# First feature tiles of a hybrid pooling and state-space block: conditioning product shared with TensorE, low parts of weights on VectorE, copies on ScalarE, written order of VectorE

## The chip, the cores and the metric

The kernel runs on one core of one Trainium2 chip. The metric is the device time of one execution in microseconds (us), the lower the better. A profile shows the span from the first to the last instruction of one execution.

## The reference, cut to what matters

The block is a decoder layer with adaptive normalization. What the change touches is the first projection and the modulation ahead of it; all is float32, with 1024 tokens and a width of 1024.

```python
c_act = silu(c)
mod = einsum('bd,de->be', c_act, w_ada) + b_ada          # 1024 -> 6 x 1024
shift_m, scale_m, gate_m, shift_f, scale_f, gate_f = split(mod, 6)
u = rms_norm(h, g_mix) * (1.0 + scale_m) + shift_m
proj = einsum('bsd,de->bse', u, w_in)                    # pooling, z, xBC, dt
...                                                       # pooling and SSD mixers, w_out
u = rms_norm(h, g_mlp) * (1.0 + scale_f) + shift_f
h = h + gate_f * (square(relu(u @ w_up)) @ w_down)
```

## The kernel before, in words

**High and low parts.** A float32 product is made of three products in a shorter format. Each operand is split into a high part (a cast) and a low part (the operand less the high part). `mm3` (L244) multiplies high by high, high by low and low by high into one bank of PSUM. The high part of a weight tile is cast by ScalarE in `unit` (L194). Its low part is a subtraction (L195), on GpSimd when `ring["pool_lo"]` is set and on VectorE otherwise.

**The stage.** The change concerns the loop over eight blocks of 128 input channels, called chunks 0 to 7 here. In chunk k, six output tiles of 128 features (B, C and four x tiles) take the first 512 tokens: 6 x 3 = 18 matmuls of 128x512 into six banks that stay open through all chunks. Chunk k needs the modulated input `u` of block k as high and low part, and the weight tile k (128x768) as high and low part. Two buffers each hold raw weight tiles, their high parts and their low parts, so the parts of tile k+2 overwrite those of tile k.

**The conditioning product.** `u` needs the shift and the scale of block k, which are 256 columns of `w_ada`. `ada_load` brings a tile of 1024x256 (1 MB) into one of three buffers, as eight slices of 128 rows. `ada_reduce` on VectorE multiplies slice j by its column of silu(c) and adds, into two accumulators (L264 for the first two slices, L266 for the other six). `ada_dve` adds the two accumulators (L358), and `ada_pe` sums over partitions on TensorE with a column of ones (L364). `ada_cols` makes shift and scale from that on VectorE (L368, L369). Then `ada_u` calls `split_u`: the high part on ScalarE (L252), the same value in float32 on VectorE (L256), and the low part on VectorE (L257).

**The order.** A planner puts each engine's instructions in order by its own costs. Under `pinned` the named engines keep the order in which the program is written. `AP[k]` says before which of the six tiles of chunk k the conditioning of block k+1 is put, and `CUTS[k]` says how many slices of block k+2 are reduced ahead of it. `stage_x` transposes the block of x for k+2 on TensorE and copies it out on ScalarE; `SX0` and `SX` give its place. After the matmuls of chunk k the next weight tile, k+2, is requested. In chunk 5 the first two of the units that follow (z and dt columns, 512 wide) are requested too, then rows 4 to 7 of x. `XS` says in which chunk those rows are normalized: rows 4 and 5 are scaled on GpSimd (L501), 6 on VectorE, 7 on ScalarE. After the stage come the z and dt products, the convolutions and the other halves of the tiles.

Of the kernel before, what the change touches and what calls it, by code (L numbers as in the profile page):

```python
# [9 lines left out]
F32 = mybir.dt.float32  # L10
F32R = mybir.dt.float32r
BF16 = mybir.dt.bfloat16
AF = mybir.ActivationFunctionType
# [4 lines left out]
P = 128  # L18
S = 1024
D = 1024  # L20
# [15 lines left out]
EPS = 1e-5  # L36
UM = 544
WARM = 7
CUTS = (0, 4, 4, 4, 4, 4, 4, 4)
UACT = ()  # L40
AP = (5, 2, 2, 2, 2, 2, 2)
UH = ((), (0,), (1, 2), (3, 4), (5, 6, 7))
XK = 5
NPF = 2
XS = {5: (4,), 6: (5, 6), 7: (7,)}
WARM2 = 2
XWB = 1
Z0 = 240
# [3 lines left out]
FIN2 = 8.0  # L52
N20 = 10.0
SX0 = 1
SX = 1
PK = 2
N21 = 15.6
G21 = 1.6
# [11 lines left out]
def tile_hybrid_block(  # L70
# [133 lines left out]
    def prefetch(n):  # L204
        while specs and len(ready) < n:
            kn, ncol, parts, gate = specs.popleft()
            ready.append(unit(kn, ncol, parts, gate() if gate is not None else None))
# [65 lines left out]
    def feat_specs(off):  # L273
        for i in range(2):
            specs.append((4, P, [(0, P, win_r[:, 4 * i:4 * i + 4, off:off + P])], None))
# [39 lines left out]
    def utmp():  # L315
        return stp.tile([P, HW], F32, name="utmp", tag="utmp", bufs=2)
# [23 lines left out]

    def ada_load(k):
        t = stp.tile([P, KD, 256], F32, name="adaw", tag="adaw", bufs=3)
        n = 4 if k == 0 else 1
        w = KD // n
        for j in range(n):
            ks = slice(j * w, (j + 1) * w)
            for f in range(2):
                sp.dma_start(out=t[:, ks, f * P:(f + 1) * P], in_=wada_r[:, ks, f * D + k * P:f * D + (k + 1) * P])
        ada_w[k] = t

    ada_a = {}

    def ada_dve(k, ks=range(KD)):
        if ks.start == 0:
            ada_a[k] = [stp.tile([P, 256], F32, name="adaa", tag="adaa", bufs=4) for _ in range(2)]
        ada_reduce(ada_w[k], ada_a[k], 256, ks)
        if ks.stop == KD:
            dve.tensor_tensor(out=ada_a[k][0], in0=ada_a[k][0], in1=ada_a[k][1], op=ALU.add)  # L358

    def ada_pe(k):  # L360
        ps = bank()
        pa, pb = ps[:, 0:1], ps[:, 1:2]
        for f, p_ in enumerate((pa, pb)):
            pe.matmul(p_, lhsT=ada_a[k][0][:, f * P:(f + 1) * P], rhs=ones[:, 0:1], start=True, stop=True)  # L364
        ada_cols(k, pa, pb)

    def ada_cols(k, pa, pb):
# [3 lines left out]
                                 in1=pc[:, C_GMIX + k:C_GMIX + k + 1], op0=ALU.add, op1=ALU.mult)  # L371

    def ada_u(k):
        uT[k][0] = split_u(stage.pop(k), sc_m[:, k:k + 1], sh_m[:, k:k + 1], utmp(), k in UACT)

    stage = {}

# [8 lines left out]
    with pinned((act, dve, pool, pe)):  # L386
# [45 lines left out]
        row_scale(3, False, slice(0, HW))  # L432
        row_scale(3, True, slice(HW, D))
        dve_f0(range(2, KD))
        dve.tensor_tensor(out=acc[0], in0=acc[0], in1=acc[1], op=ALU.add)
        for i in range(3):
            pe_f1(range(2 * i, 2 * i + 2))
            busy(2)
        stage_x(0)
        pe_f1(range(6, KD))  # L440
        pe.matmul(pa, lhsT=acc[0], rhs=ones[:, 0:1], start=True, stop=True)
        ada_cols(0, pa, pb)
        ada_u(0)
        pool.tensor_tensor(out=lo0, in0=raw0, in1=hi0.bitcast(F32), op=ALU.subtract)
        stage_x(1)
        busy(WARM2)
        kw.append([(hi0, lo0)])
# [7 lines left out]
        pool.dma_start(out=nea, in_=a_log.broadcast_to([P, HEADS]))  # L455
        pool.dma_start(out=dsk, in_=d_skip.broadcast_to([P, HEADS]))

    ring["pool_lo"] = True
    kw.append(get(1, 0))
    accs = [bank() for _ in range(6)]  # L460
    for k in range(KD):
        if k + 2 < KD:
            ada_load(k + 2)
        if k == 0:
            ada_dve(1)
        whi, wlo = kw[k][0]
        u = uT[k][0]
        for f in range(6):
            if f == (SX0 if k < 2 else SX) and k + 2 < KD:
                stage_x(k + 2)  # L470
            if k + 1 < KD and f == AP[k]:
                cut = CUTS[k]
                with pinned((dve,)):
                    if cut and k + 2 < KD:
                        ada_dve(k + 2, range(cut))
                    ada_pe(k + 1)
                    ada_u(k + 1)
                    if k + 2 < KD:
                        ada_dve(k + 2, range(cut, KD))
            fs = slice(f * P, (f + 1) * P)  # L480
            mm3(accs[f], whi[:, fs], wlo[:, fs], (u[:, 0, :], u[:, 1, :]), k == 0, k == KD - 1)
        if k == PK:
            params()
        if k + 2 < KD:
            kw.append(get(1, 0))
        if k == 5:
            ring["now"] = (unitm, unitm, UM, 4, 6)
            ring["pool_lo"] = False
            for i in range(4):
                specs.append((2, 256, [  # L490
                    (0, Z0, win_r[:, 2 * i:2 * i + 2, OFF_Z:OFF_Z + Z0]),
                    (Z0, 256, win_r[:, 2 * i:2 * i + 2, OFF_DT:OFF_DT + HEADS])], None))
            feat_specs(G1[0][0])
        if k == XK:
            prefetch(NPF)
            for t in range(4, 8):
                sp.dma_start(out=tok[:, t, :], in_=x_r[:, t, :])
        for t in XS.get(k, ()):
            row_rs(t, pool)
            if t < 6:  # L500
                pool.tensor_tensor(out=tok[:, t, :], in0=tok[:, t, :], in1=rst[:, t:t + 1].broadcast_to([P, D]),  # L501
                                   op=ALU.mult)
            else:
                row_scale(t, t == 7)
    prefetch(6)
    ring["pool_lo"] = True
    st.close()
# [1019 lines left out]
```

## Time and profile before

| | before |
|---|---|
| median of 3 runs | 1175.19 us (1174.83 to 1176.52) |
| profiled execution | 1176.13 us, span 1174.4 us |
| TensorE busy | 1138.9 us, 97% of the span |
| VectorE busy | 837.2 us, 71% |
| ScalarE busy | 558.5 us, 48% |
| GpSimd busy | 191.5 us, 16% |
| mean granted TensorE clock | 0.991 |

The profiled execution is 1.73 us longer than its span and 0.94 us above the median. A busy share over the whole span is a mean over stages. The stage of the change lies between 16.7 and 77 us, where TensorE was busy for 48.97 of 60.3 us at a mean granted clock of 0.89.

### The profile page before, as it was taken

How to read it: one execution, taken by the hardware profiler on the slowest of the kernel's cores; microseconds unless marked ns; L12 is line 12 of the kernel's file. 1: busy time of each engine (PE TensorE's matmuls, PEld its weight loads, DVE VectorE, ACT ScalarE, POOL GpSimd, SP SyncE). 2: the span in 40 equal slices, each digit the busy share in tenths (PEclk: the TensorE clock that was granted, in tenths of full speed). 3: DMA queues.
4: the chain of work that ended last, by engine and by line, in shares of the span. 5: the costliest groups of instructions: out<-in, count | busy, mean ns of one | idle time of the engine just before them, and what ended most of it. 6: DMA issues, size and time to landing. Idle time of an engine off the chain costs nothing.

```text
span 1174.4 us, 15348 instructions
## 1 busy us (share of the span) xinstructions
PE 1138.9 (97%) x5569; PEld 946.2 (81%) x5569; DVE 837.2 (71%) x1232; ACT 558.5 (48%) x977; POOL 191.5 (16%) x214
## 2 busy tenths in 40 slices
PE   6889999999999999999999999999999999999997
PEld 5678787777799988887778888888888888888886
DVE  6968879967978746664887766666566844586985
ACT  4266566544433633544764444444444444335363
POOL 4233446524500011122000000000100000000030
PEclk9989999999999999999999999999999999999999
DMA  9831342233357645853146343442399934775732
GB/s 288 234 112 37 81 137 91 73 94 103 109 186 220 201 155 172 277 170 135 37 182 237 118 189 128 168 152 108 122 388 362 338 108 151 242 250 198 268 126 90
DMA packets 124876, 200.73 MB, mean 171 GB/s; under 512 B 8416, under 2 KB 67584, under 8 KB 122752
## 3 DMA queue, kind: packets, MB, share of 16 engines
q1 hardware_dynamic: 123440, 196.24, 50.0%
q0 software_dynamic: 1120, 3.21, 0.8%
q8 instruction: 43, 0.70, 0.2%
q10 hardware_dynamic: 240, 0.30, 0.1%
q14 instruction: 33, 0.27, 0.1%
HBM read 159.81 MB, written 39.91 MB: 170 GB/s over the span
## 4 chain that ended last, share of the span: by engine, by line
PE 86%; DVE 7%; DMA 2%; ACT 2%; issue 1%; SPq 1%; POOL 1%; POOLq 0%; ACTq 0%; DVEq 0%
PE bank L244 78%; DVE cv L542 3%; PE bank L720 2%; PE bank L138 1%; PE bank L724 1%; PE bank L717 1%; DMA raw<-in_w_in_dram 1%; DMA adaw<-in_w_ada_dram 1%; DVE adaa L266 1%; PE bank L796 1%; PE bank L1003 1%; DMA tok<-in_x_dram 1%; DVE cv L553 1%; DVE lo L195 0%; POOL tok L953 0%
## 5 line engine op out<-in xcount | busy, mean ns | idle before, releaser
L244 PE MATMUL bank<-u,hi 128*128 128x512 f32 x560 | 186.2, 414 | 2.1 <-ACT u L252 2.0
L244 PE MATMUL bank<-dhi 128*128 128x512 f32 (+1 forms) x452 | 175.1, 387 | 1.1 <-DVE tmp L1423 1.1
L244 PE MATMUL bank<-dlo,dhi 128*128 128x512 f32 (+1 forms) x452 | 175.0, 387 | 0.0
L244 PE MATMUL bank<-dhi,dlo 128*128 128x512 f32 (+1 forms) x452 | 175.0, 387 | 0.0
L244 PEld LDWEIGHTS bank<-u,hi 128*128 128x128 f32 x560 | 105.3, 192 | 30.1 <-issue 5.0
L1358 DVE TENSOR_TENSOR dlo<-fr,dhi 128x1024 fp32r<-128x1024 f32 x56 | 68.4, 1222 | 82.4 <-ACT dhi L1357 82.3
L244 PE MATMUL bank<-hi,ym 128*128 128x512 f32 x384 | 125.4, 400 | 0.0
L1357 ACT CAST dhi<-fr 128x1024 fp32r<-128x1024 f32 x56 | 58.9, 1052 | 139.2 <-PE bank L244 103.9
L244 PE MATMUL bank<-u,lo 128*128 128x512 f32 x280 | 111.3, 397 | 0.0
L194 ACT CAST hi<-raw 128x512 fp32r<-128x512 f32 (+2 forms) x109 | 67.8, 630 | 91.4 <-PE bank L244 70.2
L195 DVE TENSOR_TENSOR lo<-raw,hi 128x512 fp32r<-128x512 f32 (+1 forms) x87 | 65.1, 759 | 49.7 <-ACT hi L194 49.0
L244 PEld LDWEIGHTS bank<-dhi 128*128 128x128 f32 x452 | 84.8, 188 | 18.8 <-DVE tmp L1423 1.3
L244 PEld LDWEIGHTS bank<-dhi,dlo 128*128 128x128 f32 x452 | 84.9, 188 | 17.3
L244 PEld LDWEIGHTS bank<-dlo,dhi 128*128 128x128 f32 x452 | 84.9, 188 | 17.2
L244 PE MATMUL bank<-hi,u 128*128 128x256 f32 (+1 forms) x512 | 98.2, 289 | 0.1
L179 POOL TENSOR_TENSOR rst<-ssq,mhalf 128x1 f32<-128x1 f32 (+2 forms) x27 | 27.4, 1015 | 399.5 <-DVE ssq L178 374.3
L244 PE MATMUL bank<-E,whl 128*128 128x512 f32 x384 | 91.6, 389 | 0.0
L244 PEld LDWEIGHTS bank<-hi,ym 128*128 128x128 f32 x384 | 72.1, 188 | 16.4 <-issue 0.7
L244 PEld LDWEIGHTS bank<-E,whl 128*128 128x128 f32 x384 | 72.1, 188 | 15.0
L244 PEld LDWEIGHTS bank<-hi,u 128*128 128x128 f32 x512 | 81.0, 191 | 1.3 <-issue 0.7
L244 PE MATMUL bank<-u,whl 128*128 128x512 f32 x312 | 75.2, 389 | 0.9 <-ACT whl L1137 0.9
L244 PE MATMUL bank<-lo,ym 128*128 128x512 f32 x192 | 75.3, 392 | 0.0
(254 smaller groups left out, 2159.7 us busy)
## 6 DMA issues: line engine op xcount, KB each, us to landing
f_d<-tok SPq DMA_DIRECT2D x16, 1792.0 KB, 7.2
wr<-in_w_down_dram SPq DMA_DIRECT2D x56, 512.0 KB, 5.3
fr<-f_d SPq DMA_DIRECT2D x53, 512.0 KB, 4.2
raw<-in_w_ada_dram SPq DMA_DIRECT2D x64, 256.0 KB, 3.1
wraw<-in_w_up_dram SPq DMA_DIRECT2D x16, 1024.0 KB, 5.4
raw<-in_w_in_dram SPq DMA_DIRECT2D x48, 256.0 KB, 3.0
raw<-in_w_out_dram SPq DMA_DIRECT2D x48, 256.0 KB, 3.1
tok<-in_x_dram SPq DMA_DIRECT2D x16, 512.0 KB, 6.0
```

What stands on the lines that cost most here:

```text
L138: return pe.transpose(dst, src, ident)
L179: pool.tensor_tensor(out=rst[:, a:b], in0=m, in1=mhalf[:, :b - a], op=ALU.pow)
L194: act.copy(hi[:, :n], raw[:, :n])
L195: (pool if ring.get("pool_lo") else dve).tensor_tensor(out=lo[:, :n], in0=raw[:, :n], in1=hi[:, :n].bitcast(F32), op=ALU.subtract)
L244: pe.matmul(ps, lhsT=st_, rhs=mv, start=first and i == 0, stop=last and i == 2, skip_group_check=more)
L266: dve.scalar_tensor_tensor(out=a, in0=view[:, k, :n], scalar=cact[:, k:k + 1], in1=a, op0=ALU.mult, op1=ALU.add)
L542: dve.scalar_tensor_tensor(out=v, in0=cr[:, k:k + HW], scalar=pw[:, 12 * k + ct:12 * k + ct + 1], in1=v, op0=ALU.mult, op1=ALU.add)
L553: dve.scalar_tensor_tensor(out=v, in0=th, scalar=1.0, in1=v, op0=ALU.add, op1=ALU.mult)
L717: pe.matmul(po, lhsT=C[:, cs], rhs=states[g], start=True, stop=True)
L720: pe.matmul(py[:, hh * HD:(hh + 1) * HD], lhsT=Ms[hh // 4][:, (hh % 4) * P:(hh % 4 + 1) * P], rhs=xdt[:, hh * HD:(hh + 1) * HD], start=Tru ...
L1357: act.copy(hi, src)
L1358: dve.tensor_tensor(out=lo, in0=src, in1=hi.bitcast(F32), op=ALU.subtract)
```

## The change

- `ADA_PE` takes slices of the conditioning product from VectorE to TensorE: slices 4 to 7 for blocks 1 and 2, slices 6 and 7 for block 3. TensorE multiplies each slice by a column of silu(c) into the same PSUM column.
- The sum of the two accumulators (L358, and L435 for block 0) is gone. TensorE multiplies both accumulators by ones into the same column.
- Low parts of the weight tiles 0 to 7 are made on VectorE, not on GpSimd.
- `ada_hi` and `ada_lo` take the place of `ada_u` for blocks 1 to 7. The float32 copy of `u` is on VectorE for blocks 1 to 3 (`TDVE`) and on ScalarE for blocks 4 to 7.
- The written order of VectorE now covers the whole of chunks 0 to 5, low parts of weights included, with other values of `CUTS` and `AP`. In chunks 3 to 5 the rest of the reduction stands between `ada_hi` and `ada_lo`.
- The transposes of x for blocks 4 to 7 come one tile later (`SX` 2). The load of block 1 is issued in four pieces, not in two. Rows 4 and 5 are scaled on VectorE, one chunk later for row 4, and rows 4 to 7 are divided between chunks 6 and 7.

```diff
-CUTS = (0, 4, 4, 4, 4, 4, 4, 4)
-UACT = ()
-AP = (5, 2, 2, 2, 2, 2, 2)
+CUTS = (0, 0, 0, 2, 4, 4, 0)
+TDVE = (1, 2, 3)
+AP = (4, 1, 1, 1, 1, 1, 1)
+ADA_PE = {1: (4, 5, 6, 7), 2: (4, 5, 6, 7), 3: (6, 7)}
-XS = {5: (4,), 6: (5, 6), 7: (7,)}
+XS = {6: (4, 5), 7: (6, 7)}
-SX = 1
+SX = 2
-        n = 4 if k == 0 else 1
+        n = (4, 2)[k] if k < 2 else 1
-    def ada_dve(k, ks=range(KD)):
-        if ks.start == 0:
+    def ada_dve(k, ks):
+        ks = [j for j in ks if j not in ADA_PE.get(k, ())]
+        if not ks:
+            return
+        if ks[0] == 0:
             ada_a[k] = [stp.tile([P, 256], F32, name="adaa", tag="adaa", bufs=4) for _ in range(2)]
         ada_reduce(ada_w[k], ada_a[k], 256, ks)
-        if ks.stop == KD:
-            dve.tensor_tensor(out=ada_a[k][0], in0=ada_a[k][0], in1=ada_a[k][1], op=ALU.add)
         for f, p_ in enumerate((pa, pb)):
-            pe.matmul(p_, lhsT=ada_a[k][0][:, f * P:(f + 1) * P], rhs=ones[:, 0:1], start=True, stop=True)
+            fs = slice(f * P, (f + 1) * P)
+            for j in ADA_PE.get(k, ()):
+                pe.matmul(p_, lhsT=ada_w[k][:, j, fs], rhs=cact[:, j:j + 1], start=j == ADA_PE[k][0], stop=False)
+            for i in range(2):
+                pe.matmul(p_, lhsT=ada_a[k][i][:, fs], rhs=ones[:, 0:1], start=k not in ADA_PE and i == 0,
+                          stop=i == 1)
+    def ada_hi(k):
+        u = uT[k][0] = actp.tile([P, 2, HW], F32R, name="u", tag="a")
+        tmp, src = utmp(), stage.pop(k)
+        act.activation(out=u[:, 0, :], in_=src, func=AF.Identity, scale=sc_m[:, k:k + 1], bias=sh_m[:, k:k + 1])
+        if k in TDVE:
+            dve.tensor_scalar(out=tmp, in0=src, scalar1=sc_m[:, k:k + 1], scalar2=sh_m[:, k:k + 1],
+                              op0=ALU.mult, op1=ALU.add)
+        else:
+            act.activation(out=tmp, in_=src, func=AF.Identity, scale=sc_m[:, k:k + 1], bias=sh_m[:, k:k + 1])
+        return tmp
+    def ada_lo(k, tmp):
+        u = uT[k][0]
+        dve.tensor_tensor(out=u[:, 1, :], in0=tmp, in1=u[:, 0, :].bitcast(F32), op=ALU.subtract)
-        dve.tensor_tensor(out=acc[0], in0=acc[0], in1=acc[1], op=ALU.add)
+        dve.tensor_tensor(out=lo0, in0=raw0, in1=hi0.bitcast(F32), op=ALU.subtract)
-        pe.matmul(pa, lhsT=acc[0], rhs=ones[:, 0:1], start=True, stop=True)
+        for i in range(2):
+            pe.matmul(pa, lhsT=acc[i], rhs=ones[:, 0:1], start=i == 0, stop=i == 1)
-        pool.tensor_tensor(out=lo0, in0=raw0, in1=hi0.bitcast(F32), op=ALU.subtract)
-    ring["pool_lo"] = True
-                with pinned((dve,)):
-                    if cut and k + 2 < KD:
-                        ada_dve(k + 2, range(cut))
-                    ada_pe(k + 1)
-                    ada_u(k + 1)
-                    if k + 2 < KD:
-                        ada_dve(k + 2, range(cut, KD))
+                ada_dve(k + 2, range(cut))
+                ada_pe(k + 1)
+                tmp = ada_hi(k + 1)
+                if cut:
+                    ada_dve(k + 2, range(cut, KD))
+                ada_lo(k + 1, tmp)
+                if not cut and k + 2 < KD:
+                    ada_dve(k + 2, range(KD))
-            if t < 6:
-                pool.tensor_tensor(out=tok[:, t, :], in0=tok[:, t, :], in1=rst[:, t:t + 1].broadcast_to([P, D]),
-                                   op=ALU.mult)
-            else:
-                row_scale(t, t == 7)
+            row_scale(t, t == 7)
+    with pinned((dve,)):
+        ada_dve(1, range(KD))
+        for k in range(6):
+            chunk(k)
+    chunk(6)
+    chunk(7)
```

## Rows read from the trace of the kernel before

**Rows 1.** Windows: length, busy of PE PEld DVE ACT POOL, clock, DMA, GB/s.

```profile
16.70:77.00 60.30, 48.97 (x208) 38.55 (x209) 49.50 (x96) 21.00 (x35) 23.00 (x21) 0.89 0.75 211
...
25.60:33.85 8.25, 6.85 (x26) 5.39 (x26) 7.67 (x18) 2.67 (x5) 1.88 (x1) 0.79 1.07 292
...
47.41:54.19 6.78, 5.48 (x29) 4.17 (x27) 6.35 (x14) 2.02 (x4) 2.03 (x1) 1.00 0.93 258
```

**Rows 2.** Waits between 16.7 and 77 us: total, times, longest.

```profile
PE bank L364 <- DVE adaa L358: 9.6, 5, 2.9
```

**Rows 3.** Timeline of chunk 5, VectorE: start, duration, instruction.

```profile
47.38 0.69 DVE L257 TENSOR_TENSOR u<-utmp,u 128x512 fp32r<-128x512 f32 x1 [0.36 <-ACT u L252]
47.99 3.26 DVE L266 SCALAR_TENSOR_TENSOR adaa<-adaw,cact,adaa 128x256 f32<-128x256 f32 x4
51.29 0.42 DVE L358 TENSOR_TENSOR adaa<-adaa 128x256 f32<-128x256 f32 x1
51.63 0.61 DVE L264 TENSOR_SCALAR adaa<-adaw,cact 128x256 f32<-128x256 f32 x2
52.16 0.87 DVE L266 SCALAR_TENSOR_TENSOR adaa<-adaw,cact,adaa 128x256 f32<-128x256 f32 x2
52.95 0.15 DVE L368 TENSOR_TENSOR sh_m<-bank,pc 128x1 f32<-128x1 f32 x1
...
53.26 0.55 DVE L256 TENSOR_SCALAR utmp<-stage,sc_m,sh_m 128x512 f32<-128x512 f32 x1
```

**Rows 4.** Line L266, all of the stage: duration in ns, min/median/max.

```profile
L266 DVE SCALAR_TENSOR_TENSOR adaa<-adaw,cact,adaa x42: 470/479/2075, 19.2 to 64.3; 128x256 f32<-128x256 f32 x42
```

**Rows 5.** Timeline of TensorE in chunk 5, and GpSimd beside it.

```profile
48.15 2.03 POOL L195 TENSOR_TENSOR lo<-raw,hi 128x768 fp32r<-128x768 f32 x1 [3.96 <-ACT hi L194]
...
49.14 0.40 PE L244 MATMUL bank<-u,lo 128*128 128x512 f32 x1
...
50.07 0.40 PE L244 MATMUL bank<-u,lo 128*128 128x512 f32 x1
...
53.71 0.60 PE L138 MATMUL bank<-ident,tok 128*128 128x128 f32 x4
54.19 0.50 PE L244 MATMUL bank<-u,hi 128*128 128x512 f32 x1
```

**Rows 6.** Timeline of TensorE, chunks 0 and 1, and the end of the stage.

```profile
23.76 0.58 PE L364 MATMUL bank<-ones,adaa 128*128 128x1 f32 x4 [2.75 <-DVE adaa L358]
...
28.07 0.63 PE L244 MATMUL bank<-u,hi 128*128 128x512 f32 x1
28.49 0.63 PE L244 MATMUL bank<-u,lo 128*128 128x512 f32 x1
...
69.87 0.41 PE L244 MATMUL bank<-hi,u 128*128 128x256 f32 x1
...
72.22 1.80 PE L244 MATMUL bank<-u,hi 128*128 128x512 f32 x4
```

**Rows 7.** Timeline of weight loads, block 0: products with a slice of w_ada.

```profile
13.19 0.53 PEld L428 LDWEIGHTS bank<-cact,adaw 128*128 128x128 f32 x4
13.64 0.53 PEld L333 LDWEIGHTS bank<-ones,ident 128*128 128x128 f32 x4
```

**Rows 8.** Low parts on VectorE elsewhere: duration in ns, min/median/max.

```profile
L195 DVE TENSOR_TENSOR lo<-raw,hi x6: 676/682/693, 64.7 to 81.0; 128x512 fp32r<-128x512 f32 x6
...
L1358 DVE TENSOR_TENSOR dlo<-fr,dhi x56: 1214/1224/1227, 855.5 to 1150.6; 128x1024 fp32r<-128x1024 f32 x56
```

**Rows 9.** Timeline of ScalarE in chunk 5.

```profile
53.32 0.81 ACT L252 ACTIVATE u<-stage,sh_m,sc_m 128x512 fp32r<-128x512 f32 x1 [4.76 <-DVE sc_m L369]
54.04 0.82 ACT L194 CAST hi<-raw 128x768 fp32r<-128x768 f32 x1
```

**Rows 10.** Chain of waits near the end of the stage: start, duration, piece.

```profile
56.40 7.92 DMA raw<-in_w_in_dram
```

**Rows 11.** Windows behind the stage, columns as in Rows 1.

```profile
92.00:135.00 43.00, 42.92 (x248) 37.30 (x247) 37.65 (x63) 25.80 (x48) 17.81 (x22) 1.00 0.21 56
```

More of the change, by code (lines that the diff above doesn't have):

```diff
@@ L373, in ada_u @@
     def ada_u(k):
-        uT[k][0] = split_u(stage.pop(k), sc_m[:, k:k + 1], sh_m[:, k:k + 1], utmp(), k in UACT)
+        uT[k][0] = split_u(stage.pop(k), sc_m[:, k:k + 1], sh_m[:, k:k + 1], utmp(), False)
+    def ada_hi(k):
[11 more added lines that the diff above has]
+        dve.tensor_tensor(out=u[:, 1, :], in0=tmp, in1=u[:, 0, :].bitcast(F32), op=ALU.subtract)
     stage = {}
@@ L456, in tile_hybrid_block, with chunk @@
         pool.dma_start(out=dsk, in_=d_skip.broadcast_to([P, HEADS]))
-    ring["pool_lo"] = True
     kw.append(get(1, 0))
     accs = [bank() for _ in range(6)]
-    for k in range(KD):
+    def chunk(k):
         if k + 2 < KD:
             ada_load(k + 2)
-        if k == 0:
-            ada_dve(1)
         whi, wlo = kw[k][0]
@@ L493, in tile_hybrid_block @@
             feat_specs(G1[0][0])
+            prefetch(NPF)
         if k == XK:
-            prefetch(NPF)
             for t in range(4, 8):
```

## The prediction, made before the changed kernel was run

> **What bounds the kernel now.** I first read the windows over the stage [rows 1]. The first feature tiles run from 16.7 to 77 us. In these 60.3 us TensorE is busy for 48.97 and VectorE for 49.50, and the granted clock is 0.89 on average. One chunk of the middle shows which of the two sets the pace: in 6.78 us TensorE has 5.48 us of work at clock 1.00, while VectorE's 6.35 us of merged busy time leave only the gap in which it waits for ScalarE's high part. The list of waits then names the place [rows 2]: five times, 9.6 us in all, TensorE stands at the conditioning sum (L364) until VectorE has added its two accumulators (L358).
>
> The timeline of that chunk shows VectorE's round, 47.38 to 54.16 [rows 3]. Its largest piece is four reductions that take 3.26 us, while two of them take 0.79 us (52.16 to 52.95) further on. The extreme duration of the same line is 2075 ns against a median of 479 [rows 4], and it falls beside GpSimd's low part of the weights, 2.03 us long [rows 5]. So GpSimd's work, meant to relieve VectorE, holds it up for about 1.6 us a chunk. The DMA queues come last in the reading: they were full, at 292 GB/s, for part of the stage [rows 1], but the list names no DMA among TensorE's waits.
>
> **How much there is to get.** At full clock a 128x512 matmul follows the one before it after (50.07 - 49.14) / 4 = 0.233 us, and four transposes take 54.19 - 53.71 = 0.48 us [rows 5]. Two conditioning products, four weight loads, take 13.64 - 13.19 = 0.45 us [rows 7]. The stage needs 8 x 18 x 0.233 = 33.6 us of matmuls, 6 x 0.48 = 2.9 of transposes, and 7 x 0.45 = 3.2 for 14 conditioning products. The eleven 128x256 matmuls of the next stage that the planner put inside took 72.22 - 69.87 = 2.35 us [rows 6] at the slow clock, so half of that, 1.2, at the fast one. That is 40.9 us out of 60.3. The other 19.4 are idle time and matmuls at the lower level, 1.2 GHz, where the spacing is 28.49 - 28.07 = 0.42 us [rows 6].
>
> **What the change adds on TensorE.** Blocks 1 to 7 take 12, 12, 8 and four times 4 conditioning products, 48 in place of 14. The 34 more cost 34 x 0.225 = 7.65 us, nothing hides them, and TensorE is to be the pace setter. Taken from the busy time of the same row (0.53 us for two) [rows 7] they would cost 9.0. Block 0's second product, one more in the start-up, is dropped as small. 19.4 - 7.65 = 11.75 us remain if TensorE then never waits.
>
> **VectorE's new round.** For blocks 4 to 7 it holds eight reductions, 52.16 - 51.63 = 0.53 for the first two and 6 x 0.40 for the rest, 2.9 us in all. The shift and scale take 53.26 - 52.95 = 0.31 us and the low part of `u` 47.99 - 47.38 = 0.61 [rows 3]. New is the low part of a 128x768 weight tile. The trace has it at 128x512 for 0.68 us and at 128x1024 for 1.22 [rows 8]; I take the middle, 0.95. The sum is 4.8 us, where before it was 6.78: gone are the addition (51.63 - 51.29 = 0.34), the float32 copy and the 1.6 us of blocking. Blocks 1 to 3 keep the copy, 0.55 us [rows 3], but give two or four reductions of 0.40 to TensorE, so they lie at 4.6 or below. TensorE's own round in chunks 3 to 5 is 4.19 + 0.48 + 0.90 = 5.57 us. VectorE fits under it with 0.8 us to spare; that spare time covers the low part's price, and at 1.22 it still would.
>
> **ScalarE** gets the float32 copy for blocks 4 to 7, like L252 at 0.81 us [rows 9]. It has 2.0 us of work in 6.78 [rows 1], so I cost the four copies at nothing as load. They lengthen one chain: low part of `u` later by 0.81. VectorE spends that time in the second half of the reduction (1.6 us), which covers it.
>
> **The new wait.** VectorE now makes the low part of weight tile k+2 itself. That must wait until TensorE is through with chunk k, which frees the buffer, and until ScalarE has cast the high part (0.82 us) [rows 9]. Queued behind it on VectorE are the shift and scale of block k+2 and all reductions, and TensorE waits for both. The circle in chunks 4 to 6 is: chunk 5.57, cast 0.82, low part 0.95, first half of the reduction 1.3, shift and scale 0.31, second half 1.6, low part of `u` 0.61. That is 11.2 us for two chunks, 5.6 a chunk, just above 5.57. So it nearly closes without loss, but every late step shows.
>
> **Stalls that stay.** Into chunk 1: 0.31 + 0.81 + 0.61 = 1.73 us of chain behind the sum, with six matmuls (1.4 us) to cover it, 0.35 lost. In chunk 3, TensorE comes to the sum of block 4 while its eight reductions, which start only after the low part of block 3, are running: 0.4. The circle, three chunks with 0.2 each for gaps between instructions: 0.6. Eight changes of chunk at 0.1: 0.8, an estimate by the gaps between dependent instructions in VectorE's round. Together 2.15 us. Both ends: 0.5 if the planner fills them with later matmuls, as it did before, and 5 if each of the seven rounds is late by 0.7.
>
> **Parts at nothing.** In the start-up VectorE takes the low part of weight tile 0 and loses the addition and a GpSimd neighbour: between a loss of 0.95 and a gain of about as much, taken as zero. Scaling rows 4 and 5 on VectorE costs two instructions, where GpSimd's blocked an addition for about as long; it lies beside the last chunks. Load pieces: the second half of a 1 MB load costs SP two more issues, covered by queues already full at that point. Moving the transposes one tile later costs nothing while four stage buffers are ahead. A chunk's loads are 1.05 + 0.39 MB, 4.9 us at 292 GB/s [rows 1]: under 5.57, so the DMA doesn't set the pace, but it is next in line.
>
> **Sum.** 11.75 - 2.15 = 9.6 us. From the profiled execution's 1176.13 that makes 1166.5. It lies 0.94 above the median of 1175.19, so against the median the forecast is 1165.6 us. Behind the stage, between 92 and 135 us, TensorE is busy for 42.92 of 43.0 us [rows 11], so what is gained ahead of it should arrive at the end. The forecast's own range, by 9.0 for the products and 0.5 to 5 us of stalls, is 1164 to 1170.
>
> **Rivals.**
>
> Clock falls behind the thin products (chance 0.17). Before, TensorE idled for 2.75 us and then ran four instructions of one column [rows 6]. The next window had a granted clock of 0.79 [rows 1], and about ten matmuls at 0.42. The change puts 12 products in a row, 2.7 us with almost no columns, into chunks 0 and 1, and 1.8 us into chunk 2. Against it: they do keep the engine issuing. Two to three falls of ten to twelve matmuls at 0.19 us more make 4 to 6 us: 1170.5. The Trainium skill ("TensorE: Matmul & The Clock Gate", "What's actually happening") says that the fast clock has to be earned by recent TensorE activity and the slow one is the default. By that rule I would expect these falls if thin products don't count as activity; the idle stretch above agrees with it, and no row shows what products alone do.
>
> Late raw tiles at the end (0.15). VectorE's written order ends chunk 5 with the low parts of two z units. Their raw tiles needed 7.92 us to land before [rows 10]. If they land 3 us after VectorE arrives and block 7's shift stands behind them, chunk 7 waits 3 us, and matmuls at the low clock behind it cost 2 more: 1170.6. My walk through the rounds puts VectorE there about 2 us after they land.
>
> The clock stays low through chunks 0 to 3 (0.06): the other side. All 72 matmuls there at 0.42 cost 72 x 0.19 = 13.7 us, 4.1 more than the gain: 1179.3. It decides from 9.6 / 0.19 = 50 matmuls. Against it: the clock came back behind the 2.75 us gap, and the window of chunk 5 has it at 1.00 [rows 1], with a gap in each chunk.
>
> The gain is given back behind the stage (0.07): VectorE is busy for 37.65 of 43 us there [rows 11], and its convolutions could set the time however early the tiles come: 1175, or a little over with the planner's other order.
>
> **Chances and range.** The forecast has 0.55. Faster than the median by over 0.2%, which is about what a measurement of this kernel can tell from no change: 0.55 + 0.17 + 0.15 = 0.87. Within it: 0.05, most of the last rival. Slower: 0.06 + 0.02 = 0.08. The range reaches from 1161.5, where the planner fills every gap and the start-up gains too, to 1172.5, which takes in the two rivals at 1170.5 and leaves out the last two.
>
> **What would show it.** Right: the stage's tiles end near 67 us; TensorE's waits at L364's successor sum to under 2.5 us; reductions stay near 479 ns, none near 2 us; a round lasts 5.6 us; the clock is 1.00 in chunks 3 to 7. Wrong: matmuls spaced by 0.42 in chunks 1 and 2; VectorE waiting for the cast (L194) by more than 0.8 us a chunk; products at more than 0.27 us; or the stage early and the convolutions no earlier.

## The result, and the profile after

| | before | after |
|---|---|---|
| median of 16 runs each (lowest, highest), us | 1176.37 (1174.13, 1177.45) | 1169.26 (1165.20, 1175.31) |
| profiled execution, us | 1176.13 | 1170.18 |
| span, us | 1174.4 | 1168.3 |
| VectorE busy, us | 837.2 | 823.9 |
| GpSimd busy, us | 191.5 | 169.7 |

The ratio is 0.9942 [0.9929, 0.9956]: faster by 0.6%, 7.1 us between the medians where 9.6 were forecast. The executions of the changed kernel scatter far more than those of the one before. Seven lie between 1165.2 and 1166.2, six between 1168.8 and 1171.3, three between 1173.3 and 1175.3. The profiled one is of the middle group.

The lines of the changed kernel are one higher, and further on by more: `mm3` is L245, the low part of a weight tile L196, the reductions L265 and L267, the slice products L368, the sum over the accumulators L370, shift and scale L375 and L376, the high part of `u` L386, its low part L396. First the windows (columns as in [rows 1]): the stage, two rounds of VectorE in its second half, and the stretch behind it.

```profile
16.70:77.00 60.30, 59.71 (x348) 52.02 (x347) 40.47 (x97) 31.78 (x52) 5.29 (x12) 1.00 0.81 223
...
47.30:52.65 5.35, 4.99 (x28) 3.98 (x27) 5.35 (x16) 2.84 (x4) 0.00 (x0) 1.00 0.84 219
52.65:57.50 4.85, 4.85 (x29) 4.14 (x28) 4.75 (x14) 2.83 (x4) 0.00 (x0) 1.00 1.03 261
92.00:135.00 43.00, 42.92 (x236) 36.94 (x236) 39.50 (x63) 24.98 (x48) 20.09 (x24) 1.00 0.26 68
```

In the 60.3 us of [rows 1] TensorE is now busy for 59.71 and VectorE for 40.47, where both had about 49. The list of waits over the stage says the same: the wait of [rows 2], 9.6 us, is gone, TensorE has 0.6 us of waits left up to 75 us, and VectorE is now the one that waits (total, times, longest).

```profile
DVE sh_m L375 <- PE bank L370: 11.5, 4, 5.7
...
PE bank L245 <- ACT u L386: 0.4, 1, 0.4
PE bank L245 <- DVE lo L196: 0.2, 1, 0.2
```

The reductions have lost the long one of [rows 4] (ns, min/median/max), and the low part of a weight tile at 128x768 is now on VectorE:

```profile
L267 DVE SCALAR_TENSOR_TENSOR adaa<-adaw,cact,adaa x32: 476/481/483, 20.6 to 58.9; 128x256 f32<-128x256 f32 x32
...
L196 DVE TENSOR_TENSOR lo<-raw,hi x9: 686/954/959, 28.0 to 63.2; 128x768 fp32r<-128x768 f32 x7, 128x512 fp32r<-128x512 f32 x2
```

One round of VectorE, to be held against [rows 3] (start, duration, instruction):

```profile
47.29 0.16 DVE L375 TENSOR_TENSOR sh_m<-bank,pc 128x1 f32<-128x1 f32 x1
...
47.48 2.46 DVE L267 SCALAR_TENSOR_TENSOR adaa<-adaw,cact,adaa 128x256 f32<-128x256 f32 x6
49.85 0.69 DVE L396 TENSOR_TENSOR u<-utmp,u 128x512 fp32r<-128x512 f32 x1
50.46 0.95 DVE L196 TENSOR_TENSOR lo<-raw,hi 128x768 fp32r<-128x768 f32 x1
51.33 0.61 DVE L265 TENSOR_SCALAR adaa<-adaw,cact 128x256 f32<-128x256 f32 x2
51.85 0.88 DVE L267 SCALAR_TENSOR_TENSOR adaa<-adaw,cact,adaa 128x256 f32<-128x256 f32 x2
52.65 0.15 DVE L375 TENSOR_TENSOR sh_m<-bank,pc 128x1 f32<-128x1 f32 x1
```

Six reductions take 49.85 - 47.48 = 2.37 us, 0.40 each, where four took 3.26. The round is 52.65 - 47.29 = 5.36 us and holds ten multiplications of slices (L265 and L267 together); the next, with eight, is 57.49 - 52.65 = 4.84.

**Where the time went.** For the bookkeeping I cut each profiled execution at two marks: the first 128x512 feature matmul, and the end of the last one of the stage. The time from the start of the span to the first mark is the start-up, between them lies the stage, and the rest is what lies behind.

| profiled execution | start-up | stage | TensorE waits in it | behind | time |
|---|---|---|---|---|---|
| before | 16.74 | 60.55 | 11.27 | 1097.1 | 1176.13 |
| after | 20.06 | 48.94 | 0.36 | 1099.3 | 1170.18 |

The stage is 11.6 us shorter. About 1.3 of that are the 11 products of the z columns that the planner had put inside before [rows 6] and that now lie behind (0.12 us each at the fast level; there, at the low one, they took 2.35), so 10.3 are gained. Behind the stage 2.2 us more are spent, of which the same products make 1.3. And the first matmul comes 20.06 - 16.74 = 3.3 us later. 10.3 - 3.3 - 0.9 = 6.1 us, the difference of the spans.

The start-up is where the forecast lost. TensorE's timeline of the changed kernel there:

```profile
7.88 3.19 PE L334 MATMUL bank<-ones,ident 128*128 128x128 f32 x14
10.87 0.90 PE L450 MATMUL bank<-cact,adaw 128*128 128x1 f32 x4
11.63 1.20 PE L334 MATMUL bank<-ones,ident 128*128 128x128 f32 x4
12.62 0.85 PE L450 MATMUL bank<-cact,adaw 128*128 128x1 f32 x4
...
16.89 0.85 PE L450 MATMUL bank<-cact,adaw 128*128 128x1 f32 x4
...
20.06 0.77 PE L245 MATMUL bank<-u,hi 128*128 128x512 f32 x1
20.63 1.05 PE L139 MATMUL bank<-ident,tok 128*128 128x128 f32 x4
...
22.31 0.39 PE L245 MATMUL bank<-u,lo 128*128 128x512 f32 x1
```

and that of the kernel before:

```profile
7.79 3.19 PE L333 MATMUL bank<-ones,ident 128*128 128x128 f32 x14
10.77 0.85 PE L428 MATMUL bank<-cact,adaw 128*128 128x1 f32 x4
11.49 1.08 PE L333 MATMUL bank<-ones,ident 128*128 128x128 f32 x4
12.41 0.50 PE L428 MATMUL bank<-cact,adaw 128*128 128x1 f32 x4
```

The order is the same, fillers and products of block 0 in turn, and up to 16 us TensorE pauses in neither. A filler (L334, L333) is a 128x128 matmul, in two instructions, whose result nothing reads; the kernel puts `WARM` of them behind the transpose of the parameters and two behind each of the first three pairs of block 0's products. The kernel before goes over to the fast level at about 12.3 us (four instructions of one column in 0.50), and the changed one only at about 22.3 (0.85 for such four at 16.89, and 1.05 for four transposes at 20.63, where the kernel before took 0.60). VectorE, which needs the sum of block 0 for its first shift, waits 4.15 us for it at 18.63:

```profile
18.63 0.16 DVE L375 TENSOR_TENSOR sh_m<-bank,pc 128x1 f32<-128x1 f32 x1 [4.15 <-PE bank L464]
...
27.18 0.16 DVE L375 TENSOR_TENSOR sh_m<-bank,pc 128x1 f32<-128x1 f32 x1 [5.69 <-PE bank L370]
...
34.31 0.16 DVE L375 TENSOR_TENSOR sh_m<-bank,pc 128x1 f32<-128x1 f32 x1 [2.54 <-PE bank L370]
```

### The profile page after: what moved, and what is told of

The parts are those of the page before. It is cut to its first block, busy times and chain, and to the rows that moved or that the text cites. A ratio compares the mean times of both kernels' runs of the same rounds, so it can differ in the third digit from the quotient of the medians.

```text
span 1168.3 us, 15472 instructions
## 1 busy us (share of the span) xinstructions
PE 1143.4 (98%) x5639; PEld 953.8 (82%) x5639; DVE 823.9 (71%) x1220; ACT 561.8 (48%) x981; POOL 169.7 (15%) x204
## 4 chain that ended last, share of the span: by engine, by line
PE 83%; DVE 8%; DMA 3%; ACT 3%; issue 2%; POOL 1%; POOLq 0%; SPq 0%; ACTq 0%; DVEq 0%
PE bank L245 74%; PE bank L743 2%; DMA raw<-in_w_ada_dram 2%; DVE cv L565 2%; PE bank L139 2%; PE bank L747 1%; PE bank L740 1%; DVE acc L851 1%; PE bank L334 1%; PE bank L819 1%; DVE lo L196 1%; ACT tok L905 1%; PE bank L1026 1%; POOL rst L180 0%; DMA adaa<-in_b_ada_dram 0%
## 5 line engine op out<-in xcount | busy, mean ns | idle before, releaser
L245 PE MATMUL bank<-u,hi 128*128 128x512 f32 x560 | 185.6, 411 | 0.4 <-ACT u L386 0.4
L245 PE MATMUL bank<-dhi 128*128 128x512 f32 (+1 forms) x452 | 175.1, 387 | 1.1 <-DVE tmp L1446 1.1
L245 PE MATMUL bank<-dlo,dhi 128*128 128x512 f32 (+1 forms) x452 | 175.0, 387 | 0.0
L245 PE MATMUL bank<-dhi,dlo 128*128 128x512 f32 (+1 forms) x452 | 175.0, 387 | 0.0
L245 PEld LDWEIGHTS bank<-u,hi 128*128 128x128 f32 x560 | 104.6, 191 | 28.0 <-issue 5.0
L245 PE MATMUL bank<-hi,ym 128*128 128x512 f32 x384 | 125.4, 400 | 0.0
L245 PE MATMUL bank<-u,lo 128*128 128x512 f32 x280 | 111.1, 397 | 0.0
L196 DVE TENSOR_TENSOR lo<-raw,hi 128x512 fp32r<-128x512 f32 (+2 forms) x94 | 72.2, 781 | 48.5 <-ACT hi L195 48.1
L245 PEld LDWEIGHTS bank<-dhi 128*128 128x128 f32 x452 | 84.9, 188 | 18.5 <-DVE tmp L1446 1.3
L245 PEld LDWEIGHTS bank<-dlo,dhi 128*128 128x128 f32 x452 | 84.9, 188 | 17.5
L245 PEld LDWEIGHTS bank<-dhi,dlo 128*128 128x128 f32 x452 | 84.9, 188 | 17.3
L245 PE MATMUL bank<-hi,u 128*128 128x256 f32 (+1 forms) x512 | 97.4, 288 | 0.2
L245 PE MATMUL bank<-E,whl 128*128 128x512 f32 x384 | 91.6, 389 | 0.0
L245 PEld LDWEIGHTS bank<-hi,ym 128*128 128x128 f32 x384 | 72.1, 188 | 16.4 <-issue 0.7
L245 PEld LDWEIGHTS bank<-E,whl 128*128 128x128 f32 x384 | 72.1, 188 | 15.0
L245 PEld LDWEIGHTS bank<-hi,u 128*128 128x128 f32 x512 | 80.1, 189 | 1.4 <-issue 0.7
L245 PE MATMUL bank<-u,whl 128*128 128x512 f32 x312 | 75.2, 389 | 0.8 <-ACT whl L1160 0.8
L245 PE MATMUL bank<-lo,ym 128*128 128x512 f32 x192 | 75.4, 392 | 0.0
```

The source lines that it names most:

```text
L196: (pool if ring.get("pool_lo") else dve).tensor_tensor(out=lo[:, :n], in0=raw[:, :n], in1=hi[:, :n].bitcast(F32), op=ALU.subtract)
L245: pe.matmul(ps, lhsT=st_, rhs=mv, start=first and i == 0, stop=last and i == 2, skip_group_check=more)
```

## The experiments

In each expectation theory A is the one that I held then; its rivals are B and C. Two questions were open: whether the late rise of TensorE's clock is what the gain lacks, and what each part of the change is worth. They ran in three groups, and each ratio is against the kernel before run beside it, with medians of 1175.2, 1176.0 and 1176.4 us. The profiled executions, cut as above:

| kernel | start-up | stage | TensorE waits | behind | time |
|---|---|---|---|---|---|
| before_warm | 16.77 | 57.07 | 11.58 | 1099.2 | 1174.66 |
| before_cold | 19.86 | 57.79 | 10.05 | 1096.5 | 1175.97 |
| before_dve_lo | 19.70 | 52.44 | 6.39 | 1100.2 | 1174.02 |
| after_warm | 16.42 | 51.12 | 0.19 | 1099.7 | 1169.02 |
| after_cold | 20.37 | 51.65 | 0.37 | 1099.0 | 1172.77 |
| after_pool_lo | 20.20 | 56.77 | 2.11 | 1099.5 | 1178.21 |
| after_dve | 20.49 | 46.26 | 1.65 | 1098.8 | 1167.62 |
| after_warm_dve | 18.29 | 49.92 | 3.15 | 1098.9 | 1168.96 |
| after_dve_fill | 16.35 | 49.26 | 3.64 | 1099.9 | 1167.38 |
| after_dve_fill2 | 22.19 | 45.24 | 1.65 | 1099.0 | 1168.23 |
| after_thick | 22.08 | 46.04 | 0.00 | 1099.8 | 1169.82 |
| after_dve_copies | 20.24 | 47.63 | 1.65 | 1100.2 | 1170.09 |

The stages of before_warm and before_cold hold the 11 products of the z columns too, that of before_dve_lo 9, that of after_dve_copies 4, the others none.

**after_warm: twelve fillers ahead of the start-up of the changed kernel.**

```diff
     with pinned((act, dve, pool, pe)):
+        busy(12)
         row_rs(0)
```

> The changed kernel with 12 filler matmuls of 128x128 at the head of TensorE's order, before the transpose of the parameters, where it idled from about 2.3 to 7.5 us. Theory A (TensorE gets its fast level late in the start-up, and the changed stage, which TensorE now paces, cannot make the delay up): the conditioning products of block 0 run at the fast spacing (about 0.5 us for four, not 0.85), the first feature matmul starts by 17 us, not at 20.06, and the median falls to 1163 to 1166 us with runs within 2 us of each other. Rival B (the missing microseconds and the scatter come from the stage itself: conditioning products, DMA landings or the planner's order): the median stays within 1 us of 1169 and the scatter of some 10 us stays.

Measured: 1169.15 us (1165.34 to 1174.27, 6 runs), ratio 0.9939 [0.9919, 0.9960]. Theory A held for the first matmul, which came at 16.42, 3.6 us earlier than in the changed kernel, and missed the median, which did not move. In the profile the clock fell later, among the products of block 2 (windows, then timeline of TensorE):

```profile
25.00:30.00 5.00, 5.00 (x32) 4.71 (x32) 2.40 (x7) 1.21 (x2) 0.00 (x0) 0.84 1.13 303
30.00:35.00 5.00, 5.00 (x13) 3.86 (x12) 3.35 (x8) 1.19 (x2) 0.00 (x0) 0.50 1.15 304
```

```profile
21.05 0.58 PE L370 MATMUL bank<-ones,adaa 128*128 128x1 f32 x4
...
25.67 0.95 PE L368 MATMUL bank<-cact,adaw 128*128 128x1 f32 x8
...
27.63 1.16 PE L368 MATMUL bank<-cact,adaw 128*128 128x1 f32 x8
28.65 0.99 PE L370 MATMUL bank<-ones,adaa 128*128 128x1 f32 x4
29.50 1.20 PE L245 MATMUL bank<-u,hi 128*128 128x512 f32 x2
```

TensorE does not idle there. The eight instructions at 25.67 take 0.95 us, those at 27.63 take 1.16, the next four 0.99 where four of the same kind took 0.58 at 21.05, and from 30 to 35 us only 13 instructions run, at clock 0.50. This is the first rival of the prediction, seen, and one of the causes that rival B here had named.

**before_warm: the same line in the kernel before.**

> The kernel before with the same 12 filler matmuls. Theory A: VectorE paces its stage and waits for the second block of w_ada until 18.6 us anyway, so an earlier fast level is worth under 1.5 us: 1174 to 1176 us. Rival B says nothing of the start-up: no change.

Measured: 1176.0 us (1174.61 to 1177.39, 11 runs), ratio 1.0000 [0.9991, 1.0009]. As expected, nothing. But the run says little about an earlier start, since its first matmul comes at 16.77, where the profile of the kernel before has 16.74: in both TensorE waits 0.34 us there for ScalarE's high part. The other direction, below, says more.

**after_cold and before_cold: no fillers ahead of block 0's products.**

```diff
-WARM = 7
+WARM = 0
```

> The changed kernel without the seven filler matmuls behind the transpose of the parameters (WARM 0), so that the fast level comes later. Theory A: the first feature matmul starts at 20 us or later in the profile, and the median is 1169 to 1172 us, with the early runs near 1165 us gone. Rival B: no change, 1169 with the same scatter.

> The kernel before without the seven fillers. Theory A: VectorE's round takes up about half of a 3 us delay, so 1 to 2 us slower than before: 1176 to 1179 us. Rival B: no change.

Measured: after_cold 1170.83 us (1170.39 to 1172.77, 5 runs), ratio 0.9959 [0.9947, 0.9971]; before_cold 1176.28 (1175.74 to 1177.67, 11 runs), ratio 1.0007 [0.9998, 1.0016]. Without the fillers none of five executions of the changed kernel reaches the group at 1165 to 1166, where seven of sixteen were. That points to the fillers, and so to an early rise, as what the group needs; five runs are few to prove it. The kernel before loses 0.8 us by the ratio, whose interval takes in no change, although its first matmul comes 19.86 - 16.74 = 3.1 us later: at the end of the stage 0.36 us of that is left (77.65 against 77.29). TensorE's waits shrank by 1.2 us, and it spent less of the stage at the low level behind its waits (mean granted clock between 16.7 and 77 us 0.94, before 0.89). The profile of after_cold has the late start (20.37) and a stretch at clock 0.50 between 30 and 35 us as well, and is the slowest of its five.

**after_dve: no slice products on TensorE.**

```diff
-ADA_PE = {1: (4, 5, 6, 7), 2: (4, 5, 6, 7), 3: (6, 7)}
+ADA_PE = {}
```

> The changed kernel with ADA_PE empty and no early fillers. Theory A: the late first rise remains in some runs, the fall behind the products doesn't: 1163 to 1169 us, and none of the slowest runs near 1174. Rival B: as the changed kernel, 1165 to 1175. Rival C: slower than the changed kernel by 2 to 5 us.

Measured: 1163.74 us (1163.01 to 1167.62, 5 runs), ratio 0.9907 [0.9894, 0.9920]. This beats both kernels: 12.3 us under the kernel before on the same chip. No execution lies above 1167.62, which is the profiled one, and that one has a late start (20.49). The fastest of it and of the changed kernel are 1163.0 and 1165.2. Part of the 5.5 us to the median of the changed kernel is that four of these five executions, at 1163.0 to 1164.6, were of the early kind, and only seven of the sixteen there. In the profiles, both with a late start, the stage is 2.7 us shorter: 20 products less at 0.21 us are 4.2, and one wait of 1.28 us comes in. Even with all slices VectorE still waits for TensorE's sum in four rounds of the stage, two of them below. The wait of 1.28 us is not VectorE's lateness either: ahead of it TensorE made the sum last in its chunk, VectorE had waited 0.86 us for that sum, and TensorE then had nothing to cover shift, scale and the high part.

```profile
16.70:77.00 60.30, 58.27 (x330) 50.16 (x330) 46.69 (x111) 32.84 (x54) 5.39 (x13) 1.00 0.82 230
```

```profile
25.84 0.16 DVE L375 TENSOR_TENSOR sh_m<-bank,pc 128x1 f32<-128x1 f32 x1 [2.33 <-PE bank L370]
...
32.89 0.16 DVE L375 TENSOR_TENSOR sh_m<-bank,pc 128x1 f32<-128x1 f32 x1 [0.86 <-PE bank L370]
```

```profile
34.13 1.43 PE L245 MATMUL bank<-u,hi 128*128 128x512 f32 x5 [1.28 <-ACT u L386]
```

**after_warm_dve: after_dve with the twelve fillers.** The edits of after_warm and after_dve together.

> The changed kernel with the 12 early fillers and with no slice of the conditioning product on TensorE (ADA_PE empty): VectorE reduces all eight slices of every block, and TensorE loses 20 thin products. Theory A (the runs of one-column products let TensorE's clock fall): no stretch with 0.42 us between matmuls in chunks 1 and 2, median 1161 to 1165 us and runs within 3 us of each other. Rival B (the clock falls there whatever TensorE runs): a low stretch in chunk 1 or 2 as before, median 1165 to 1170. Rival C (the shared products are needed because VectorE's eight reductions come too late in chunks 0 to 2): TensorE waits at the sum for over 1.5 us per chunk there, 1167 or slower.

Measured: 1168.96 us (1165.88 to 1169.96, 5 runs), ratio 0.9940 [0.9928, 0.9953]. Theory A missed; the time is in the ranges of B and C, for reasons that neither names in full. The fast level came early (the 14 instructions of the seven fillers took 1.73 us, not 3.19), was lost at about 13.7 us among block 0's products, and again at about 48.5, behind a wait. TensorE waits 1.22 us for VectorE's reduction and 1.45 for ScalarE's high part in the stage.

**after_pool_lo: low parts of the weight tiles back on GpSimd.**

```diff
+    ring["pool_lo"] = True
     kw.append(get(1, 0))
```

> The changed kernel with the low parts of weight tiles 1 to 7 back on GpSimd. Theory A (GpSimd's low part holds VectorE up for 1.6 us a chunk): single reductions of some 2 us reappear, VectorE's round in chunks 3 to 5 goes from 4.8 to about 5.5 us, and the kernel is 1 to 4 us slower than the changed one. Rival B (TensorE paces, so VectorE's round doesn't matter): within 1 us of the changed kernel.

Measured: 1171.41 us (1168.09 to 1178.21, 12 runs), ratio 0.9970 [0.9951, 0.9988]; the fastest is 2.9 us above the fastest of the changed kernel. This is within theory A. The long reduction is back, and the multiplication of the first two slices has a long one too:

```profile
L267 DVE SCALAR_TENSOR_TENSOR adaa<-adaw,cact,adaa x32: 465/476/2071, 20.7 to 67.5; 128x256 f32<-128x256 f32 x32
...
L265 DVE TENSOR_SCALAR adaa<-adaw,cact x14: 340/347/1940, 19.6 to 63.5; 128x256 f32<-128x256 f32 x14
```

The profile is of the slowest of the twelve and must not be read as the price of GpSimd: its stage of 56.77 us also has TensorE at the low level from about 27 to 37 us, busy throughout. The fall began among the slice products, as in after_warm.

```profile
30.00:35.00 5.00, 5.00 (x19) 4.21 (x19) 1.71 (x5) 1.32 (x2) 0.22 (x1) 0.50 0.56 152
```

**before_dve_lo: that one part alone, in the kernel before.**

```diff
-    ring["pool_lo"] = True
     kw.append(get(1, 0))
```

> The kernel before with only the low parts of weight tiles 1 to 7 moved from GpSimd to VectorE. Theory A: each round of VectorE loses 1.6 us of being held up and gains 0.95, 0.65 in seven rounds: 4 to 5 us faster, 1170 to 1172 us. Rival B (being held up is not what the long reductions show): the round grows by 0.95, 5 to 7 us slower.

Measured: 1172.85 us (1171.24 to 1175.05, 11 runs), ratio 0.9977 [0.9968, 0.9986], less than expected. The extreme of the reductions falls to 485 ns, VectorE's round from 6.78 to 51.48 - 45.10 = 6.38 us, and in the round stands a new wait for ScalarE's cast:

```profile
L266 DVE SCALAR_TENSOR_TENSOR adaa<-adaw,cact,adaa x42: 476/480/485, 20.6 to 62.2; 128x256 f32<-128x256 f32 x42
```

```profile
45.10 0.15 DVE L368 TENSOR_TENSOR sh_m<-bank,pc 128x1 f32<-128x1 f32 x1
...
46.76 0.96 DVE L195 TENSOR_TENSOR lo<-raw,hi 128x768 fp32r<-128x768 f32 x1 [0.80 <-ACT hi L194]
...
51.48 0.16 DVE L368 TENSOR_TENSOR sh_m<-bank,pc 128x1 f32<-128x1 f32 x1
```

Its profile tells one more thing. The code of its start-up is that of the kernel before, and yet the low level lasted until the feature matmuls, and the first of them came at 19.70, not 16.74:

```profile
12.69 0.85 PE L428 MATMUL bank<-cact,adaw 128*128 128x1 f32 x4
...
19.70 0.77 PE L244 MATMUL bank<-u,hi 128*128 128x512 f32 x1
```

So when the rise comes differs between executions (or chips, since the two ran apart) with the same start-up.

**after_dve_fill and after_dve_fill2: after_dve with more fillers.** The first has twelve at the head and `WARM = 11`; the second has four fillers in place of two behind each of the first three pairs of block 0's products.

```diff
             pe_f1(range(2 * i, 2 * i + 2))
-            busy(2)
+            busy(4)
```

> No slice of the conditioning product on TensorE (ADA_PE empty), 12 early fillers, and 11 fillers in place of 7 behind the transpose of the parameters, so that TensorE has no gap before block 0's products. Theory A (what is left is the clock in the start-up): fast spacing from about 8 us on, first feature matmul by 17.5 us, median 1160 to 1163 us and runs within 2 us of each other. Rival B (the clock in the start-up is not what is left): within 1 us of the 1163.74 that the version without fillers had.

> ADA_PE empty, no early fillers, but four fillers in place of two behind each pair of block 0's one-column products. Theory A: the clock rises within that stretch in most runs; the six more fillers cost 6 x 0.23 = 1.4 us at the fast level, so 1163 to 1165 us with no run above 1167. Rival B: slower than 1163.74 by the fillers' 1.4 to 2.6 us and scattered as before.

Measured: after_dve_fill 1167.92 us (1167.38 to 1169.80, 5 runs), ratio 0.9935 [0.9923, 0.9947]; after_dve_fill2 1167.25 (1166.32 to 1168.23, 4 runs), 0.9925 [0.9912, 0.9937]. Both missed. after_dve_fill starts its first matmul at 16.35, and TensorE then waits for VectorE's reduction, with low clock behind the wait:

```profile
21.78 0.38 PE L370 MATMUL bank<-ones,adaa 128*128 128x1 f32 x2 [1.71 <-DVE adaa L267]
...
45.15 1.20 PE L245 MATMUL bank<-u,hi 128*128 128x512 f32 x4 [1.45 <-ACT u L386]
```

```profile
20.00:25.00 5.00, 3.29 (x19) 2.74 (x18) 3.02 (x7) 1.15 (x2) 0.00 (x0) 0.88 1.15 303
25.00:30.00 5.00, 5.00 (x22) 4.04 (x20) 4.02 (x10) 1.32 (x2) 0.00 (x0) 0.78 1.13 302
```

The DMA queues move 303 GB/s in these windows, and an earlier start meets the loads: ScalarE's cast of a weight tile waits 1.60 us for the tile, VectorE's low part 1.37 for the cast, and the last two reductions, for which TensorE waits, stand behind it in VectorE's order. In after_dve_fill2 the fast level was there only at about 20 us, and the added fillers only made the start-up longer (22.19).

**after_thick: 20 fillers of 128x128 where the 20 slice products stood.**

```diff
-ADA_PE = {1: (4, 5, 6, 7), 2: (4, 5, 6, 7), 3: (6, 7)}
+ADA_PE = {}
+FILL = {1: 4, 2: 4, 3: 2}
...
-            for j in ADA_PE.get(k, ()):
-                pe.matmul(p_, lhsT=ada_w[k][:, j, fs], rhs=cact[:, j:j + 1], start=j == ADA_PE[k][0], stop=False)
+            busy(FILL.get(k, 0))
```

> ADA_PE empty, and in place of the 20 slice products of blocks 1 to 3, 20 filler matmuls of 128x128, which take TensorE about as long (0.22 us each) but stream 128 columns. Theory A (the thin products cost their time and, in some runs, the clock as well): the time comes back but not the falls: median 1165 to 1168 us, no run above 1171. Rival B (only their time counts): like the changed kernel, 1169 with runs up to 1175.

Measured: 1169.69 us (1165.34 to 1170.33, 6 runs), ratio 0.9932 [0.9916, 0.9948]. Inconclusive. The planner put five of the twenty fillers (ten instructions) ahead of chunk 0, which made the start-up 22.08; the stage has no wait and no granted clock below 1.00, and no run lies above 1170.33, but the median is the changed kernel's.

**after_dve_copies: after_dve with every float32 copy on VectorE.**

```diff
-TDVE = (1, 2, 3)
+TDVE = (1, 2, 3, 4, 5, 6, 7)
```

> ADA_PE empty, and the float32 copy of u on VectorE for all blocks (TDVE 1 to 7). Theory A (VectorE's round of 4.8 us fits under TensorE's with room): its round grows to some 5.3 us in chunks 3 to 6, 0 to 2 us slower than 1163.74. Rival B (the copies on ScalarE stand on the path, since the low part of u is later by 0.81 us): up to 1 us faster.

Measured: 1169.20 us (1164.59 to 1170.09, 6 runs), ratio 0.9932 [0.9916, 0.9947]. Between the profiles the stage is 47.63 - 46.26 = 1.4 us longer, about 0.5 of it the four products of z columns that the planner put inside; between the fastest executions it is 1.6. The 5.5 us between the medians lie within the scatter of executions, so the size stays open. Nothing here supports rival B, that the copies on ScalarE cost time.

## Why the prediction was right, and where it was off

The time lies inside the range, 3.7 us above the forecast, on the side of faster. Of the 3.7, 1.2 are the kernel before, whose median is 1176.37 here and was 1175.19 for the forecast. Seven of the sixteen executions lie within 0.7 us of the forecast's 1165.6; the others are later, and the median falls between the groups. That two terms were off in opposite directions, the stalls and the start-up, and that the range had room for rivals that cost as much, is luck and not foresight.

**The mechanism held.** GpSimd's low part held VectorE up: with it on VectorE no reduction is near 2 us, in either kernel, and with it back on GpSimd the 2071 ns return. This part is worth about 3 us: before_dve_lo gains 3.2 in the median, and after_pool_lo loses 2 to 3, though the intervals of its ratio and of the changed kernel's touch (0.9951 to 0.9988, 0.9929 to 0.9956). So most of the 10.3 us belongs to the rest of the change, of which the sum without an addition, the written order of VectorE and the later transposes were not separated by any run.

**VectorE's round and the new wait.** The low part was taken as 0.95 and took 0.954 us. The round was summed to 4.8 with eight slices, and the round with eight is 4.84. The circle of 5.6 us did not show: TensorE waits for 0.36 us in the stage where 2.15 were summed. The term of stalls was 1.8 us too large.

**Products on TensorE.** 34 at 0.225 us were summed. In the changed kernel the twelve instructions from 24.41 to 25.66 are six products, 0.21 each:

```profile
24.41 0.95 PE L368 MATMUL bank<-cact,adaw 128*128 128x1 f32 x8
25.21 0.58 PE L370 MATMUL bank<-ones,adaa 128*128 128x1 f32 x4
25.66 1.03 PE L368 MATMUL bank<-cact,adaw 128*128 128x1 f32 x8
```

The term is right in size. What it leaves out is the clock.

**The stage** came to a gain of 10.3 us against 9.6 summed, although the low level of its first matmuls cost 1.1 (20.06 to 22.31 for three matmuls and four transposes, 1.18 at the fast level). Its tiles ended at 69.0 us, where 67 was expected, with a start 3.3 later.

**The step that was mis-sized** stands under "Parts at nothing": the start-up, a loss of 0.95 to a gain of as much, taken as zero. It measured a loss of 3.3 us in the profiled execution, because the fast level came at 22.3 and not at 12.3. The edit of block 0 is not shown to be the cause of the late rise: before_dve_lo has the old code, rises late too and starts its first matmul at 19.70. The 0.36 us from there to 20.06 are about what block 0's second product takes at the low level, which the forecast dropped as small. What the change did was to take away the cover. In the kernel before, taking the fillers out moved the first matmul by 3.1 us in the profile and the median by about 1 us (before_cold), because VectorE was the pace setter and TensorE made the time up in its waits. Now TensorE waits for 0.36 us in the stage and has nothing to make up; that a late start therefore goes through to the end is argued from the parts below.

**The rivals.** The first, clock falls behind the thin products, happened in some executions: three of the four profiles that have slice products, after_warm, after_cold and after_pool_lo, show it (30 to 35 us at clock 0.50, with no wait ahead of it in the stage of over 0.2 us), and that of the changed kernel doesn't. Of the six without them none has such a fall in the stage without a longer wait ahead of it. That is strong for so few profiles, but not proof. The second did not happen: the low parts of the z units start at 61.63, behind the last shift. The third and the fourth did not; behind the stage at most 0.9 us came back.

**The three groups.** From the parts: an early start of 16.4, the changed kernel's stage without the slow first matmuls (48.94 - 1.1), 1099.3 behind and 1.9 around the span give 1165.4; the late start gives the 1170.18 of the profile; a late start with a low stretch gives 1172.8 (after_cold). The middle has a second way: an early start with a low stretch is 1169.02 (after_warm). These are near the three groups, and the slowest three have a mean clock of 0.993 against 0.994 to 0.998. This is argued from parts of different kernels: no execution near 1165 was profiled.

**Two theories fell.** That an earlier rise gives the missing 3 to 5 us: three kernels with an earlier first matmul (after_warm, after_warm_dve, after_dve_fill) lost it again to the clock or to waits for VectorE and the loads. And that VectorE needs the help: without the slice products the kernel is faster by 2.2 us in the fastest execution and by 2.6 between the two profiles with a late start. The 5.5 in the median also hold how many executions started early, and the kernels built on after_dve, with medians of 1167 to 1170, did not repeat it. What sets the moment of the first rise stays open.

## What to carry to other kernels

A delay that an engine makes up in its waits shows in the time as soon as that engine sets the pace: before costing a start-up at nothing, ask which slack covers it and whether the change removes that slack. Moving work onto the engine that will set the pace has to be weighed against what the relieved engine has spare afterwards: here VectorE, with all its slices back, still waited for TensorE in four rounds, and the slice products given to TensorE cost about 2 us. And when executions of one kernel scatter by 10 us, one profile shows one of them, so compare medians and fastest runs beside it.

## What the runs showed of the hardware

TensorE can run without a pause and stay at the low level: from 7.88 to 22.3 us in the changed kernel, with fillers of 128x128 and instructions of one column. And it can fall to it without a pause, among the slice products of block 2 (after_warm, 30 to 35 us at 0.50). The Trainium skill ("TensorE: Matmul & The Clock Gate", "What's actually happening") says that the low level is the default which activity releases, and that the point of the rise differs from run to run of one kernel, by 0.5 us either way. The traces agree that it differs, and by much more: with the same start-up the rise came at about 12.3 us (before) and 22.5 (before_dve_lo), and the first matmul at 16.74 and 19.70. Which work counts as activity no run here settles.

The granted clock of a window is 1.00 from 10 to 22 us in the changed kernel although four one-column products take 0.85 us there and 0.58 later: the row doesn't show the low level there, and the durations do. In after_warm_dve, where the fast level came first and was lost at 13.7, the row has 0.50 from 15 to 20 us.

While GpSimd makes a subtraction of 2.03 us, a VectorE reduction with two operands in SBUF is held up: its 479 ns become 2075 and 2071 at most in the two kernels that have both, and stay at 483 and 485 in two that don't. The multiplication with one such operand (L265) is held up as well, 1940 ns at most for 347 in after_pool_lo. The Trainium skill ("SBUF — State Buffer", "SBUF: two separate sides") calls this an exclusive lock on a shared pair of ports; for the reduction the traces agree.
